# Hybrid decoder step on one core: seven block products in place of eight for gate and up in the first and the last FFN phase

## The chip, the core and the metric

The kernel runs on one core of a Trainium2 chip. The metric is device time in microseconds (us) of one execution, given as the median of several runs. TensorE multiplies, VectorE, ScalarE and GpSimd work element by element, and DMA engines move data between HBM and SBUF; SyncE issues nearly all transfers.

## The reference, cut to what is computed

One layer for 1024 prompt rows and 8 single-token rows (samples), model width 1024, FFN width 2816, all in fp32. Both groups share the weights.

```python
def swiglu(x, w_gate, w_up, w_down):
    return (jax.nn.silu(x @ w_gate) * (x @ w_up)) @ w_down

def decoder_layer(x, ...):
    h = x + 0.5 * rmsnorm(swiglu(rmsnorm(x, n_ffn1_pre), ffn1_gate, ffn1_up, ffn1_down), n_ffn1_post)
    proj = rmsnorm(h, n_mix_pre) @ w_in
    ya = ...      # differential attention with a paged cache for the samples
    yb = ...      # RWKV-7 time mixing
    h = h + rmsnorm(jnp.concatenate([ya, yb], axis=-1) @ w_out, n_mix_post)
    h = h + 0.5 * rmsnorm(swiglu(rmsnorm(h, n_ffn2_pre), ffn2_gate, ffn2_up, ffn2_down), n_ffn2_post)
    return h, k, v, s_new, shift_new
```

## The kernel before

**Phases.** Activations lie transposed: model or FFN columns on the partitions, rows (tokens) along the free axis. The two FFNs times two halves of the rows give four phases, `ph` 0 to 3: FFN 1 on the first 520 and on the last 512 rows, then FFN 2 on the other two. Phases 0 and 3 stand at the start and at the end of the span and work on two chunks of 256 and 264 rows; phases 1 and 2 take 512 rows at a time and share the middle of the span with projections, attention and time mixing, which other streams supply.

**One product.** Fp32 accuracy comes from splitting: each operand is a high part (rounded to fp32r) and a low part (the rest), and `mm3` issues three fp32r matmuls per block of 128 rows of the weight: high x high, high x low, low x high. A gate or up product of one column tile (128 of the 2816 columns, `f` = 0 to 21) sums over 8 such blocks, 24 matmuls per chunk.

**Weights.** The stream `s_weights` loads a column tile of 512 KB into one of two raw buffers (`wts_raw`), and `split` makes the high part with a cast on ScalarE and the low part with a subtraction on VectorE or GpSimd: `either` takes the one that by the planner's prices is free first. The parts go into one of four buffers `w0` to `w3` (`wts_w` in the trace) in phases 0 and 3, after the signal `used` of the buffer's last tenant. `plan` gives the sequence: groups of two or three column tiles, gate and up for each tile, and behind the first tile of a group the down products of the group before.

**The trunk.** `s_trunk` runs the products. In `gate`, ScalarE takes tanh(g/2) of the PSUM result and VectorE forms g(1 + tanh); `up` multiplies by the up product, ScalarE casts the high part, `either` makes the low part. In phase 0 the input is not yet normalized: the gate result is multiplied by `rb` (the reciprocal norm of each row) on VectorE before the tanh, and g once more by `rb` on GpSimd, so that the up product gets its norm too. `down` sums over the tiles of a group and adds into `ytile` (`trunk_xl` in the trace). The last group of a phase is its tail: with each result, `square_sum` adds up the squares for the norm behind the FFN, and in phase 3 `s_end` turns the results back and writes them out.

**Order.** Each engine's instructions are ordered before the kernel runs by a list scheduler (`Kern.run`): streams offer their next instruction, `price` costs it, and the one with the earliest latest-start time (`late`, from a dry pass, plus `BIAS` of its stream) goes first. The order is fixed in the program; on the chip each engine follows it and waits on semaphores. The fences of rows below show pieces of that order.

## Time and profile before

| | before |
|---|---|
| median of 3 runs | 2362.34 us (2361.39 to 2362.57) |
| the profiled execution | 2372.71 us |
| span of its instructions | 2371.0 us |
| mean granted TensorE clock | 0.983 |
| TensorE busy | 2284.7 us, 96% |
| VectorE busy | 1432.8 us, 60% |
| ScalarE busy | 1012.4 us, 43% |
| GpSimd busy | 913.6 us, 39% |

The trace and its rows come from the one profiled execution; its time holds the span and 1.7 us around it. The granted clock is a share of full speed, 1.00 being 2.4 GHz. A busy TensorE is not TensorE at its peak, and a share over the whole span averages phases with different limits. In a trace `trunk` names the FFN trunk, `wts` its weights, `mix` the time mixing, `end` the output, `pre` the split inputs; a name such as `trunk_m` is a PSUM bank.

### The profile page before, as it was taken

To read this page: it belongs to the slowest core of one execution; us is meant where nothing else is said; L and a number is where in the kernel's file an instruction comes from. 1 tells how busy PE (TensorE), PEld (TensorE's weight loads), DVE (VectorE), ACT (ScalarE), POOL (GpSimd) and SP (SyncE) were. 2 spreads that over 40 slices of the span, in tenths; PEclk is the share of its full clock that TensorE was granted. 3 is DMA by queue.
4 is the path that set the end of the run, shared out by engine and by line. 5 is a ranking of instruction groups with operands and counts; after the bars stand their busy time and mean duration, and the time that the engine had idled before them with its cause. 6 is when DMAs were issued, how large, how long until landed. Compare 5 with 4: busy or idle time off the path is not lost.

```text
span 2371.0 us, 42298 instructions
## 1 busy us (share of the span) xinstructions
PE 2284.7 (96%) x16207; PEld 2039.5 (86%) x16207; DVE 1432.8 (60%) x3118; ACT 1012.4 (43%) x1967; POOL 913.6 (39%) x735
## 2 busy tenths in 40 slices
PE   7999999999999999999799989999999999999998
PEld 7999999898887777888788867777778989999998
DVE  5554445856667876648866567555677576334444
ACT  5532223544453245444542154443575564322224
POOL 4542222533433864445642133333443464111112
PEclk9999999999999999999889999999999999999999
DMA  6332233444343664635546942323544535322332
GB/s 206 121 96 88 87 93 112 140 140 132 108 125 109 205 204 138 182 114 167 149 132 182 203 113 76 90 72 92 154 140 119 172 97 146 111 84 87 91 97 73
DMA packets 461698, 299.09 MB, mean 126 GB/s; under 512 B 81177, under 2 KB 428925, under 8 KB 461496
## 3 DMA queue, kind: packets, MB, share of 16 engines
q1 hardware_dynamic: 460888, 294.78, 42.9%
q8 instruction: 128, 2.10, 0.4%
q0 software_dynamic: 320, 1.08, 0.1%
q14 instruction: 74, 0.61, 0.1%
q10 hardware_dynamic: 288, 0.52, 0.1%
HBM read 254.86 MB, written 41.46 MB: 125 GB/s over the span
## 4 chain that ended last, share of the span: by engine, by line
PE 79%; DVE 8%; ACT 5%; DMA 4%; issue 2%; POOL 1%; SPq 1%; DVEq 0%; ACTq 0%; POOLq 0%
PE trunk_m L296 50%; PE proj_m L296 10%; PE trunk_aux L296 5%; PE job_aux L296 4%; PE outb_m L296 2%; PE attn_m L296 2%; PE out_m L296 2%; DVE mix_T L296 1%; PE attn_aux L296 1%; ACT mix_X L296 1%; SPq L296 1%; ACT wts_w L296 1%; ACT mix_T L296 1%; DVE trunk_xl L296 1%; PE job_dec L296 1%
## 5 line engine op out<-in xcount | busy, mean ns | idle before, releaser
L296 PE MATMUL trunk_m<-pre_X,wts_w 128*128 128x256 f32 (+2 forms) x3264 | 556.4, 325 | 8.9 <-ACT pre_sq L296 3.5
L296 PEld LDWEIGHTS trunk_m<-pre_X,wts_w 128*128 128x128 f32 x3264 | 462.3, 193 | 50.0 <-issue 5.5
L296 PE MATMUL trunk_m<-trunk_xl,wts_w 128*128 128x256 f32 (+2 forms) x2856 | 475.6, 320 | 13.5 <-DVE trunk_xl L296 10.7
L296 ACT CAST wts_w<-wts_raw 128x1024 fp32r<-128x1024 f32 (+1 forms) x288 | 281.4, 978 | 441.6 <-PE trunk_m L296 343.9
L296 POOL TENSOR_TENSOR wts_w<-wts_raw,wts_w 128x1024 fp32r<-128x1024 f32 (+1 forms) x130 | 293.7, 2259 | 450.4 <-ACT wts_w L296 368.4
L296 PE MATMUL trunk_m<-pre_T,wts_w 128*128 128x256 f32 (+2 forms) x2592 | 452.9, 329 | 8.5 <-DVE wts_w L296 6.9
L296 PEld LDWEIGHTS trunk_m<-trunk_xl,wts_w 128*128 128x128 f32 x2856 | 403.9, 191 | 51.4 <-DVE trunk_xl L296 13.7
L296 PEld LDWEIGHTS trunk_m<-pre_T,wts_w 128*128 128x128 f32 x2592 | 375.0, 189 | 47.6 <-DVE wts_w L296 7.7
L296 DVE TENSOR_TENSOR trunk_xl<-trunk_xl,trunk_m 128x256 f32<-128x256 f32 (+2 forms) x314 | 155.8, 502 | 122.7 <-PE trunk_m L296 121.9
L296 DVE TENSOR_TENSOR wts_w<-wts_raw,wts_w 128x1024 fp32r<-128x1024 f32 (+1 forms) x158 | 185.9, 1176 | 68.8 <-ACT wts_w L296 68.0
L296 POOL TENSOR_TENSOR trunk_xl<-trunk_t,trunk_xl 128x256 fp32r<-128x256 f32 (+2 forms) x90 | 98.8, 1098 | 267.6 <-ACT trunk_xl L296 267.4
L296 PE MATMUL proj_m<-tail_xl,lin_w 128*128 128x256 f32 (+1 forms) x1248 | 165.1, 287 | 0.0
L296 PEld LDWEIGHTS proj_m<-tail_xl,lin_w 128*128 128x128 f32 x1248 | 153.5, 188 | 7.7 <-issue 6.1
L296 PE MATMUL proj_m<-tail_T,lin_w 128*128 128x512 f32 (+1 forms) x672 | 153.2, 388 | 4.8 <-DVE tail_T L296 4.8
L296 PEld LDWEIGHTS proj_m<-tail_T,lin_w 128*128 128x128 f32 x672 | 123.5, 195 | 32.7 <-DVE tail_T L296 5.5
L296 ACT CAST trunk_xl<-trunk_t 128x256 fp32r<-128x256 f32 (+2 forms) x131 | 61.2, 467 | 112.0 <-DVE trunk_t L296 68.1
L296 POOL TENSOR_TENSOR trunk_g<-trunk_g,init_rb 128x256 f32<-128x256 f32 (+1 forms) x44 | 41.3, 939 | 126.6 <-ACT trunk_t L296 126.6
L296 DVE TENSOR_TENSOR trunk_t<-trunk_g,trunk_m 128x512 f32<-128x512 f32 (+2 forms) x78 | 43.4, 557 | 76.0 <-PE trunk_m L296 73.5
L296 DVE SCALAR_TENSOR_TENSOR trunk_g<-trunk_t,trunk_m 128x512 f32<-128x512 f32 (+2 forms) x78 | 43.4, 557 | 72.8 <-ACT trunk_t L296 72.5
L296 PE MATMUL trunk_aux<-pre_T,wts_w 128*128 128x264 f32 (+1 forms) x672 | 86.8, 284 | 0.0
L296 PEld LDWEIGHTS trunk_aux<-pre_T,wts_w 128*128 128x128 f32 x672 | 83.4, 189 | 0.1
L296 POOL TENSOR_TENSOR mix_T<-mix_T 128x512 f32<-128x512 f32 x32 | 38.0, 1189 | 89.1 <-DMA mix_T<-PT 89.1
(497 smaller groups left out, 3469.9 us busy)
## 6 DMA issues: line engine op xcount, KB each, us to landing
wts_raw<-in_ffn_gate_dram SPq DMA_DIRECT2D x88, 512.0 KB
wts_raw<-in_ffn_up_dram SPq DMA_DIRECT2D x88, 512.0 KB
wts_raw<-in_ffn_down_dram SPq DMA_DIRECT2D x96, 384.0 KB
lin_raw<-in_w_in_dram SPq DMA_DIRECT2D x26, 512.0 KB
mix_T<-PT SPq DMA_DIRECT2D x37, 256.0 KB
wts_raw<-in_ffn_down_dram SPq DMA_DIRECT2D x16, 512.0 KB
dec_dreg<-in_cache_k_dram SPq DMA_DIRECT2D x32, 256.0 KB
dec_dreg<-in_cache_v_dram SPq DMA_DIRECT2D x32, 256.0 KB
```

The source lines that it names most:

```text
L296: o = Op(eng, lambda: fn(*a, **k), st)
```

## The change

`FAST = {0: 10, 3: 6}`: from column tile 10 of phase 0 and tile 6 of phase 3 on, two neighbouring tiles are a pair, and gate and up of a pair are done as a 2x2 block product with seven block multiplications (Strassen's form as Winograd wrote it). The blocks are the two tiles (a11, a12 the halves of the first over the 1024 rows of the weight, a21, a22 of the second) and the input by halves of the model width and by two halves of 260 rows. A block product is 4 blocks of 3 matmuls of 260 columns. Five streams change:

- `s_combine`, new, forms four sums of input blocks per phase: 40 additions or subtractions, 16 casts and 16 low parts of 260 columns, into `dreg`, `T2` and `T3`.
- `s_weights`: a pair's two tiles are loaded as before; `sums` makes from them four fillings of a weight buffer per kind, the first with a11 and a12, the second with the sums s2 and a11 - a21, the third with a22 and s1, the fourth (half full) with a12 - s2. s1 and s2 are written by VectorE to the PSUM banks `cb` and `dec`. Raw buffers come in two pairs in turn (`four`). All casts and low parts of the fast downs and of the sums are of 512 columns (`PARTS = 2`).
- `seven`, new: the seven products and their 14 additions per pair on VectorE, gate and up element work on blocks of 260 rows. The trunk has six PSUM banks there.
- Groups: phase 0 has [0,1,2], [3,4], [5,6,7], [8,9] and six pairs, phase 3 [0,1,2], [3], [4,5] and eight pairs. Before, both ended with a group of three.
- Phase 0 no longer multiplies g by `rb` on GpSimd. The FFN's output then lacks one factor of `rb` per row, which the norm behind it takes out, but for its epsilon: squares are scaled by `TINY`, and `s_tail` multiplies by `rb` three times on VectorE.
- `BIAS` has new values for streams of the middle as well.

```diff
+FAST = {0: 10, 3: 6}
+HALF = 260
...
-BIAS = {"trunk2": 300, "outn3": -60, "outb0": 30, "pre2": -3}
+BIAS = {"trunk2": 300, "outn3": -70, "outb0": 30, "pre2": 7, "prep1": 60, "resid0": -60, "outn1": -10, "pre3": 30, "outn0": 3, "pre1": 3, "job13": 60, "ldxb0": -60}
...
+    def sums(self, ph, kind, f, j, tag, last):
...
+        if tag in last:
+            yield ("wait", last[tag])
+        hl = self.T(self.wp, [P, 2048], tag, FR)
...
+        elif j == 1:
+            s1, s2 = self.ps(bank="cb"), self.ps(bank="dec")
+            V.tensor_tensor(s1, a21, a22, ALU.add)
+            V.tensor_tensor(s2, s1, a11, ALU.subtract)
+            put(0, s2)
+            V.tensor_tensor(a12, a12, s2, ALU.subtract)
+            self.either("tensor_tensor", a11, a11, a21, ALU.subtract)
+            put(1, a11)
+            ab.append(s1)
...
-                    G.tensor_tensor(g, g, rb, ALU.mult)
...
+                    for n, (j, i, x) in enumerate(((0, 0, b11), (0, 1, b21), (1, 0, t2), (1, 1, t3), (2, 0, t4), (2, 1, t1), (3, 0, b22))):
+                        wh, wl = yield from weights(kind, f, j)
+                        ps = self.ps(HALF)
+                        for k in range(4):
+                            self.mm3(ps, wh[:, i, k, :], wl[:, i, k, :], x[0][k], x[1][k], k == 0, k == 3)
...
+                        if n == 0:
+                            A.copy(v[0], ps)
+                        elif n == 5:
+                            V.tensor_tensor(v[2], v[2], ps, ALU.add)
+                            V.tensor_tensor(v[0], v[0], ps, ALU.add)
+                        else:
+                            o, a = ((1, 0), (0, 0), (2, 0), (3, 2), (0, 0), (0, 0))[n - 1]
+                            V.tensor_tensor(v[o], v[a], ps, ALU.add)
...
+        if ph == 0:
+            rb = self.rb[:, o:o + n]
+            for _ in range(2):
+                nc.vector.tensor_tensor(acc, acc, rb, ALU.mult)
+        self.rstd(acc, 2, 1.0 if ph else TINY ** -2)
+        if ph == 0:
+            nc.vector.tensor_tensor(acc, acc, rb, ALU.mult)
```

The order on TensorE, in the last phase before the change: the end of the down products of a group and the first rows of a gate product. `pre_T` is the input, its two numbers the high and the low part; `trunk_m` a PSUM bank; one weight filling (`wts_w_2632`) serves both chunks.

```order
L296 MATMUL trunk_aux_2648_23843<-trunk_xl_837_7957,wts_w_2626_23663 128x264 x9
L296 MATMUL trunk_m_2649_23854<-trunk_xl_837_7957,wts_w_2626_23663 128x256 x9
L296 MATMUL trunk_m_2652_23868<-pre_T_2188_19398,wts_w_2632_23716 128x264
L296 MATMUL trunk_m_2652_23868<-pre_T_2189_19399,wts_w_2632_23716 128x264
L296 MATMUL trunk_m_2652_23868<-pre_T_2188_19398,wts_w_2632_23716 128x264 x2
L296 MATMUL trunk_m_2652_23868<-pre_T_2189_19399,wts_w_2632_23716 128x264
```

And after it, for a pair: each block product is 12 matmuls on half a filling of the weights (`comb` is a sum of input blocks, `pre_T` a block of the input itself).

```order
L301 MATMUL trunk_m_2747_23058<-comb_dreg_20421,wts_w_2731_22949 128x260 x12
L301 MATMUL trunk_m_2748_23077<-comb_T_2435_20422,wts_w_2731_22949 128x260 x12
L301 MATMUL trunk_aux_2752_23097<-comb_T_2436_20423,wts_w_2737_22988 128x260 x12
L301 MATMUL trunk_aux_2753_23114<-comb_dreg_20421,wts_w_2737_22988 128x260 x12
L301 MATMUL trunk_m_2755_23138<-pre_T_2321_19678,wts_w_2740_23009 128x260
L301 MATMUL trunk_m_2755_23138<-pre_T_2322_19679,wts_w_2740_23009 128x260
L301 MATMUL trunk_m_2755_23138<-pre_T_2321_19678,wts_w_2740_23009 128x260 x2
```

A filling of a weight buffer that served 48 matmuls of gate or up serves 24 (12 for the fourth) behind the change.

The order on VectorE in the last phase before: three additions of down products, then gates, the low parts of weight fillings (1024 columns), and ups.

```order
L296 TENSOR_TENSOR trunk_xl_1556_14256<-trunk_xl_1556_14256,trunk_m_2593_23269 128x256
L296 TENSOR_TENSOR trunk_xl_1556_14256<-trunk_xl_1556_14256,trunk_m_2594_23281 128x264
L296 TENSOR_TENSOR trunk_xl_1556_14256<-trunk_xl_1556_14256,trunk_aux_2595_23292 128x256
L296 SCALAR_TENSOR_TENSOR trunk_g_23327<-trunk_t_23328,trunk_m_2598_23306 128x264
L296 SCALAR_TENSOR_TENSOR trunk_g_23327<-trunk_t_23328,trunk_m_2601_23337 128x256
L296 TENSOR_TENSOR wts_w_2602_23358<-wts_raw_23301,wts_w_2602_23358 128x1024
L296 TENSOR_TENSOR trunk_t_23328<-trunk_g_23327,trunk_aux_2604_23368 128x264
L296 TENSOR_TENSOR trunk_xl_837_7957<-trunk_t_23328,trunk_xl_837_7957 128x264
L296 TENSOR_TENSOR trunk_t_23328<-trunk_g_23327,trunk_m_2605_23398 128x256
L296 TENSOR_TENSOR wts_w_2606_23419<-wts_raw_23359,wts_w_2606_23419 128x1024
L296 SCALAR_TENSOR_TENSOR trunk_g_23450<-trunk_t_23451,trunk_m_2608_23430 128x264
```

And after, where one pair's downs end and the next pair's gates begin: `rows_X` and `init_E` are the places in which block products are summed, `wts_cb` and `wts_dec` the PSUM banks of s1 and s2.

```order
L301 TENSOR_TENSOR trunk_xl_1702_14632<-trunk_xl_1702_14632,trunk_aux_2887_24143 128x256
L301 TENSOR_TENSOR rows_X_2366_20050<-rows_X_2366_20050,trunk_m_2894_24172 128x260
L301 TENSOR_TENSOR wts_w_2895_24179<-wts_lraw_24145,wts_w_2895_24179 128x512
L301 TENSOR_TENSOR rows_X_2366_20050<-rows_X_2366_20050,trunk_m_2896_24187 128x260
L301 TENSOR_TENSOR wts_cb_24216<-wts_LT_24146 128x512
L301 SCALAR_TENSOR_TENSOR trunk_g_24156<-trunk_sq_24195,rows_X_2366_20050 128x260
L301 TENSOR_TENSOR wts_dec_24217<-wts_cb_24216,wts_lraw_24145 128x512
L301 TENSOR_TENSOR init_E_109<-rows_X_2366_20050,trunk_m_2898_24207 128x260
L301 TENSOR_TENSOR init_E_109<-init_E_109,trunk_m_2902_24227 128x260
L301 TENSOR_TENSOR wts_w_2899_24215<-wts_dec_24217,wts_w_2899_24215 128x512
L301 TENSOR_TENSOR wts_lraw_24145<-wts_lraw_24145,wts_dec_24217 128x512
L301 TENSOR_TENSOR init_E_109<-init_E_109,trunk_aux_2903_24244 128x260
```

In place of one low part of 1024 columns to a filling there are sums and low parts of 512, and between them stand the additions of the block products.

The order on TensorE at the end of the program, where the last group's down products are interleaved with the transposes of the output (`end`); before, a group of three tiles, 9 matmuls to a result:

```order
L296 MATMUL trunk_m_2673_24116<-trunk_xl_837_7957,wts_w_2656_23920 128x264 x9
L296 MATMUL trunk_m_2676_24130<-trunk_xl_837_7957,wts_w_2656_23920 128x264 x9
L296 MATMUL trunk_aux_2678_24144<-trunk_xl_837_7957,wts_w_2660_23981 128x264 x9
L296 MATMUL trunk_m_2680_24158<-trunk_xl_837_7957,wts_w_2660_23981 128x264 x5
L296 MATMUL end_m_2674_24123<-init_ident_69,trunk_xl_1556_14256 128x128
L296 MATMUL end_aux_2675_24124<-init_ident_69,trunk_xl_1556_14256 128x128
L296 MATMUL trunk_m_2680_24158<-trunk_xl_837_7957,wts_w_2660_23981 128x264
L296 MATMUL end_m_2674_24123<-init_ident_69,trunk_xl_1556_14256 128x128
L296 MATMUL end_aux_2675_24124<-init_ident_69,trunk_xl_1556_14256 128x128
```

And after, a group of two tiles, 6 matmuls to a result:

```order
L301 MATMUL trunk_aux_2999_24993<-trunk_xl_978_8303,wts_w_2977_24810 128x264 x6
L301 MATMUL trunk_m_3002_25004<-trunk_xl_978_8303,wts_w_2977_24810 128x264 x6
L301 MATMUL trunk_m_3004_25015<-trunk_xl_978_8303,wts_w_2977_24810 128x264 x6
L301 MATMUL trunk_aux_3006_25029<-trunk_xl_978_8303,wts_w_2977_24810 128x264 x3
L301 MATMUL end_m_3000_24994<-init_ident_69,trunk_xl_1702_14632 128x128
L301 MATMUL end_aux_3001_24995<-init_ident_69,trunk_xl_1702_14632 128x128
L301 MATMUL trunk_aux_3006_25029<-trunk_xl_978_8303,wts_w_2977_24810 128x264 x3
L301 MATMUL trunk_m_3008_25040<-trunk_xl_978_8303,wts_w_2980_24833 128x264 x2
L301 MATMUL end_m_3000_24994<-init_ident_69,trunk_xl_1702_14632 128x128
```

The transposes stand behind the same number of results, with fewer matmuls between them.

## Rows read from the trace of the kernel before

**Rows 1.** The page's parts 1 and 2: busy time in us, share of the span and count of instructions of each engine, and then busy tenths of TensorE and the granted TensorE clock in 40 equal slices of the span.

```profile
PE 2284.7 (96%) x16207; PEld 2039.5 (86%) x16207; DVE 1432.8 (60%) x3118; ACT 1012.4 (43%) x1967; POOL 913.6 (39%) x735
...
PE   7999999999999999999799989999999999999998
...
PEclk9999999999999999999889999999999999999999
```

**Rows 2.** Windows: stretch in us from the start of the span and its length, busy us of TensorE, of its weight loads, of VectorE, ScalarE and GpSimd with the count of instructions, then mean granted clock, mean DMA share and GB/s. The first two lie in the first FFN phase, the others in the last; windows left out between them read alike.

```profile
200.00:260.00 60.00, 60.00 (x504) 60.00 (x503) 27.79 (x54) 16.96 (x26) 14.35 (x14) 1.00 0.32 94
260.00:320.00 60.00, 60.00 (x501) 60.00 (x501) 27.00 (x54) 16.36 (x24) 15.69 (x13) 1.00 0.31 94
...
2100.00:2160.00 60.00, 60.00 (x500) 59.88 (x498) 26.65 (x51) 14.89 (x24) 10.72 (x8) 1.00 0.30 89
2280.00:2340.00 60.00, 60.00 (x501) 60.00 (x500) 21.62 (x43) 15.28 (x26) 10.69 (x8) 1.00 0.26 82
```

**Rows 3.** The chain that ended last, in order of time, near the end of the span: start in us, us, engine, what is written, line, and the count of instructions in the piece.

```profile
2323.86 5.77 PE trunk_m L296 x48
2329.63 2.92 PE trunk_aux L296 x24
2332.55 5.75 PE trunk_m L296 x48
2338.31 2.84 PE trunk_aux L296 x24
```

**Rows 4.** Windows of the middle of the span, columns as in rows 2.

```profile
480.00:800.00 320.00, 314.17 (x2698) 273.02 (x2697) 208.22 (x627) 136.60 (x275) 125.86 (x98) 1.00 0.45 129
800.00:1120.00 320.00, 308.49 (x1647) 256.01 (x1645) 216.93 (x460) 139.28 (x290) 177.98 (x125) 0.98 0.55 165
1120.00:1200.00 80.00, 65.58 (x427) 61.78 (x427) 63.66 (x124) 41.71 (x80) 44.55 (x47) 0.81 0.48 135
1200.00:1520.00 320.00, 304.05 (x1768) 237.23 (x1766) 203.33 (x428) 125.13 (x215) 105.69 (x72) 0.98 0.55 141
1520.00:1840.00 320.00, 311.47 (x1926) 251.13 (x1926) 217.34 (x588) 164.18 (x399) 121.89 (x78) 0.99 0.40 112
```

**Rows 5.** The timeline of VectorE alone in the last phase: start us, duration us, engine, line, operation, out<-in, shapes, and in brackets the idle time before it and what ended it.

```profile
2105.66 1.22 DVE L296 TENSOR_TENSOR wts_w<-wts_raw,wts_w 128x1024 fp32r<-128x1024 f32 x1
2106.80 0.41 DVE L296 TENSOR_TENSOR trunk_xl<-trunk_xl,trunk_aux 128x256 f32<-128x256 f32 x1
2107.13 0.76 DVE L296 TENSOR_TENSOR trunk_xl<-trunk_xl,trunk_m 128x264 f32<-128x264 f32 x2
2108.31 0.43 DVE L296 TENSOR_TENSOR trunk_xl<-trunk_xl,trunk_aux 128x264 f32<-128x264 f32 x1 [0.42 <-PE trunk_aux L296]
```

**Rows 6.** Groups of instructions over the whole span, shapes kept apart: engine, operation, names, shapes, count, then busy us and mean ns of one, then the idle time before them and what ended it.

```profile
L296 DVE TENSOR_TENSOR trunk_xl<-trunk_xl,trunk_m 128x512 f32<-128x512 f32 x96 | 65.4, 683 | 51.5 <-PE trunk_m L296 51.1
L296 DVE TENSOR_TENSOR mix_T<-mix_T 128x512 f32<-128x512 f32 x24 | 19.4, 807 | 2.8 <-ACT mix_T L296 2.8
L296 DVE SCALAR_TENSOR_TENSOR mix_T<-mix_T,setup_cols,mix_T 128x512 f32<-128x512 f32 x24 | 22.7, 946 | 1.2 <-POOL mix_T L296 1.2
L296 POOL TENSOR_TENSOR mix_T<-mix_T 128x512 f32<-128x512 f32 x32 | 38.0, 1189 | 89.1 <-DMA mix_T<-PT 89.1
L296 POOL TENSOR_TENSOR trunk_xl<-trunk_t,trunk_xl 128x512 fp32r<-128x512 f32 x31 | 44.6, 1439 | 45.2 <-ACT trunk_xl L296 45.0
L296 ACT CAST trunk_xl<-trunk_t 128x512 fp32r<-128x512 f32 x37 | 22.8, 617 | 3.7 <-DVE trunk_t L296 3.6
```

**Rows 7.** The same view of GpSimd alone, 2040 to 2340 us.

```profile
L296 POOL TENSOR_TENSOR trunk_xl<-trunk_t,trunk_xl 128x256 fp32r<-128x256 f32 x12 | 15.9, 1322 | 51.3 <-ACT trunk_xl L296 51.3
L296 POOL TENSOR_TENSOR trunk_xl<-trunk_t,trunk_xl 128x264 fp32r<-128x264 f32 x14 | 10.6, 757 | 130.0 <-ACT trunk_xl L296 130.0
```

**Rows 8.** The same view of ScalarE alone, 2040 to 2340 us.

```profile
L296 ACT CAST trunk_xl<-trunk_t 128x264 fp32r<-128x264 f32 x18 | 7.4, 413 | 40.8 <-DVE trunk_t L296 40.8
L296 ACT ACTIVATE trunk_t<-trunk_m 128x264 f32<-128x264 f32 x13 | 5.1, 392 | 22.9 <-PE trunk_m L296 14.9 <-POOL trunk_xl L296 8.0
```

**Rows 9.** Timelines of ScalarE and of GpSimd in the last phase, columns as in rows 5: two casts of a weight's high part, and the low part that GpSimd makes after the second.

```profile
2104.57 1.06 ACT L296 CAST wts_w<-wts_raw 128x1024 fp32r<-128x1024 f32 x1 [4.53 <-PE trunk_m L296]
2110.47 1.05 ACT L296 CAST wts_w<-wts_raw 128x1024 fp32r<-128x1024 f32 x1 [4.84 <-PE trunk_aux L296]
...
2111.60 2.38 POOL L296 TENSOR_TENSOR wts_w<-wts_raw,wts_w 128x1024 fp32r<-128x1024 f32 x1 [10.00 <-ACT wts_w L296]
```

**Rows 10.** TensorE's waits, by what released it: us in total, times, longest us. These are the three rows in which a weight's parts were waited for.

```profile
PE trunk_m L296 <- DVE wts_w L296: 9.8, 5, 4.6
PE trunk_m L296 <- POOL wts_w L296: 1.3, 1, 1.3
PE trunk_m L296 <- ACT wts_w L296: 0.8, 2, 0.4
```

**Rows 11.** The first piece of the chain that ended last.

```profile
1.96 6.36 DMA wts_raw<-in_ffn_gate_dram
```

**Rows 12.** A window over the last group of down products (its first matmul starts at 2341.14), columns as in rows 2.

```profile
2341.14:2363.50 22.36, 22.29 (x189) 21.63 (x187) 13.03 (x29) 16.89 (x37) 9.06 (x12) 1.00 0.14 49
```

**Rows 13.** Windows near the start of the span, and behind the end of the first phase.

```profile
40.00:90.00 50.00, 48.80 (x404) 48.16 (x404) 23.04 (x53) 25.93 (x52) 19.75 (x21) 0.99 0.58 194
440.00:480.00 40.00, 40.00 (x244) 35.71 (x243) 30.54 (x38) 25.61 (x49) 19.96 (x21) 1.00 0.43 129
```

More of the change, by code (lines that the diff above doesn't have):

```diff
@@ L557, in split @@
         h, l = (hl[:, 1024 * j:1024 * j + n] for j in range(2))
-        self.nc.scalar.copy(h, raw)
-        self.either("tensor_tensor", l, raw, h.bitcast(F32), ALU.subtract)
+        for i in range(0, n, n // parts):
+            t = slice(i, i + n // parts)
+            self.nc.scalar.copy(h[:, t], raw[:, t])
+            self.either("tensor_tensor", l[:, t], raw[:, t], h[:, t].bitcast(F32), ALU.subtract)
         return [t.rearrange("p (a b) -> p a b", a=a) for t in (h, l)]
@@ L772, in plan @@
             for q, f in enumerate(grp):
-                seq += [("gate", f, None), ("up", f, None)]
+                if f < FAST.get(ph, NF):
+                    seq += [("gate", f, None), ("up", f, None)]
+                elif q == 0:
+                    seq += [(kind, f, j) for kind in ("gates", "ups") for j in range(4)]
                 if gi and q == 0:
@@ L798, in s_weights @@
                     yield ("wait", ("outw", 1))
-                raw = self.raw()
+                if kind[-1] == "s":
+                    yield from self.sums(ph, kind, f, m0, tag, last)
+                    continue
+                fast = kind == "down" and groups[f][-1] + 1 >= FAST.get(ph, NF + 1)
+                if fast and not FOUR:
+                    self.side = 1
+                raw = self.four(m0 // 512) if fast else self.raw()
                 w = I[f"ffn{1 + ph // 2}_{kind}"]
@@ L924, in s_trunk @@
                 for q, f in enumerate(grp):
+                    if f >= FAST.get(ph, NF):
+                        if q == 0:
+                            if f == FAST[ph]:
+                                yield ("wait", ("combined", ph))
+                                self.cur.banks = tuple(f"m{j}" for j in range(4)) + ("aux0", "aux1")
+                                rest = [self.rest[:, HALF * i:HALF * i + HALF] for i in range(4)] if ph else [r[:, i, :] for _ in range(2) for r in [self.residual(HALF)] for i in range(2)]
+                                self.vs = [t[:, HALF * i:HALF * i + HALF] for t in (self.E, self.prb) for i in range(2)] + [self.la[:, :HALF], self.sg[:, :HALF]] + rest
+                                self.nv = 0
+                            yield from seven(f)
+                            yield from down(gi - 1, False)
+                        continue
                     if ph == 1 and f == LEAD:
@@ L954, in s_pre @@
             if c == 0:
-                x = self.x[ph] = self.parts(ph, *self.two(half))
+                tiles = self.two(half)
+                x = self.x[ph] = self.parts(ph, *tiles)
+                self.xt[ph] = [t.rearrange("p (k t) -> p k t", t=520) for t in tiles]
             for k in range(KT):
```

178 lines of the change are left out of this document (152 added, 26 removed).

## The prediction

> **What bounds the kernel now.** I read four views in this order. The page's busy shares and slices come first: TensorE is busy 96% of the span and VectorE 60% [rows 1], and the slices say where TensorE is not full. Then windows over the two stretches that the change touches: in the first FFN phase (here 200 to 380 us) and in the last (2040 to 2340 us) TensorE is busy 60.00 of every 60 us at full granted clock, VectorE 22 to 28, ScalarE 15 to 17, GpSimd 10 to 16, the DMA engines about 0.3 [rows 2]. Third, the chain that ended last runs there through matmuls alone, 48 and 24 at a time without a piece of another engine between [rows 3]. So in both stretches the end is set by the count of matmuls, and a matmul that goes away is worth its issue interval. Fourth, the middle: between 480 and 1840 us TensorE is idle 56 of 1360 us, and the granted clock falls below full where it idles [rows 4]; the change does not edit that part, but its order moves.
>
> **What is removed.** A pair of FFN column tiles had 2 tiles x 2 products x 8 blocks of rows x 3 passes x 2 chunks = 192 matmuls for gate and up; seven block products of 4 x 3 matmuls, twice, are 168. There are 6 pairs in the first phase (tiles 10 to 21) and 8 in the last (6 to 21): 14 x 24 = 336 matmuls less, all of 260 columns on average as before. Down products keep their count. From rows 3, 5.77 + 2.92 + 5.75 + 2.84 = 17.28 us for 144 matmuls is 0.120 us each, so 336 are **40.3 us**, as long as TensorE stays full.
>
> **What has to keep up, per pair.** TensorE needs 168 + 96 down matmuls = 264 x 0.120 = 31.7 us for a pair (34.6 before).
>
> VectorE: in the new order of the last phase there stand, per pair, 16 instructions of 512 columns (weight sums and low parts) and 39 of 256 to 264 columns (14 additions of block products, 16 down evictions, 4 gates, 4 ups, a low part). Back to back it starts the next instruction 1.14 us after one of 1024 columns and 0.33 us after one of 256 [rows 5], so about 1.05 ns a column: 0.60 us for 512. That is 16 x 0.60 + 39 x 0.34 = 23 us; by mean durations (0.68 and 0.81 us for 512 [rows 6], 0.43 for the small ones [rows 5]) it is at most 16 x 0.81 + 39 x 0.43 = 30 us. The first phase has four more small ones (1.4 us). GpSimd has about 10.7 instructions of 512 columns and 3.2 of 260 a pair: 10.7 x 1.19 to 1.44 [rows 6] + 3.2 x 0.76 to 1.32 [rows 7] = 15 to 20 us. ScalarE has 18.6 casts of 512 at 0.62 [rows 6] and 10 short ones of about 0.4 [rows 8]: 16 us. All are under 31.7, so no engine but TensorE is full; VectorE at its upper bound is close.
>
> No row shows VectorE writing PSUM, which 4 sums a pair now do. From below it is the 0.68 us of a 512-column addition that reads PSUM, from above the slowest VectorE row of 512 columns, 0.95 us [rows 6]. I take 0.68, since the operands are as many; the upper end adds 4 x 0.27 = 1.1 us of VectorE a pair, which the 31.7 us cover; without cover 15 us in all.
>
> **The weight buffers turn faster.** Four buffers are refilled in turn. Before, three others stood between (3 x 48 matmuls = 17 us); now they are 24, 24 and 12 matmuls at the tightest, 60 x 0.120 = 7.2 us. A refill ran from release to ready in 2.3 us where VectorE made the low part (cast starts at 2104.57, low part ends at 2106.88) and in 3.5 us with GpSimd (2110.47 to 2113.98) [rows 5, 9]. Now there are two casts and two low parts of half the size, for the second buffer also a sum in front: 2.9 to 5 us. That fits into 7.2 with 2 to 4 us for queueing. Before, TensorE waited 11.9 us in all for weights [rows 10], over 288 refills 0.041 us each; 140 refills at that rate are **5.8 us**, which I take, between 0 and the 20 us that 0.14 us each would make. The loads behind them are the same bytes; DMA is at a third [rows 2], a load at the crowded start landed in 6.4 us [rows 11], and a pair of raw buffers is asked for some 11 us before its use. Nothing for it.
>
> **The ends.** The last group of down products had three tiles, now two: the tail's matmuls drop from 144 to 96, 5.8 us that move ahead and are not lost. But in the 22.4 us of that tail ScalarE was busy 16.9 us and TensorE 22.3 [rows 12]. TensorE's share falls to 16.5, so ScalarE's 16.9 plus the wait for the first sum and its gaps (about 2 us) sets the end: 19 in place of 16.5, **+2.5 us** (0 to 4). At the end of the first phase three multiplications by rb of 0.43 us join the path to the residual; the next phase's first products fill it as now (40.00 of 40 us busy after 440 [rows 13]), so nothing, or 1.3 us without that cover. GpSimd's multiplication of the gate by rb goes, and nothing waited for it in [rows 2].
>
> Forming the four sums of x takes 56 additions and 16 casts of 260 columns a phase, 24 us if all 56 were VectorE's at 0.43, in stretches where both are under half busy and TensorE full, ahead of tile 10 and tile 6. Nothing, as long as it ends by then; in the first phase eight of these instructions come in the first 90 us, where TensorE is not full [rows 13]: 0 to 3 us, taken as 0 since TensorE waits there for others.
>
> **The middle.** New BIAS values reorder it. I take 0, with 10 us either way: one stretch, 1120 to 1200 us, alone has 14.4 us of idle TensorE and a mean clock of 0.81 [rows 4], and so much can be won or lost by an order.
>
> **The sum.** The profiled execution took 2372.71 us (span 2371.0 and 1.7 around it), 10.4 above the median of 2362.34. 2372.7 - 40.3 + 5.8 + 2.5 = 2340.7 for such an execution; less 10.4, **2330 us**.
>
> **A rule that speaks against it.** GpSimd's subtraction of 264 columns takes 0.76 us in the last phase, the same on 256 columns 1.32 [rows 7]: the second kind falls together with VectorE's 1.22 us weight subtraction, and stretches. The Trainium skill, SBUF — State Buffer, section SBUF: two separate sides, says that VectorE with two SBUF inputs and GpSimd exclude each other for a whole instruction; by that rule, and the stretched row agrees, the new mix would cost waiting on both engines. Taken as a mechanism of this kernel it is the second rival below.
>
> **Rivals.**
> (a) *Refills come late.* If a refill is late by 0.14 to 0.25 us on average, 20 to 35 us of the 40 are lost: 2344 to 2359. For it: 7.2 us in place of 17, a fixed order on VectorE. Against: at least 2 us to spare.
> (b) *VectorE and GpSimd block each other and VectorE becomes the bound; slower.* Per pair GpSimd holds 15 us, VectorE needs 23, of which 17 instructions (about 8 us) have two SBUF inputs. If VectorE stood still for more than 34.6 - 23 = 11.6 us of GpSimd's 15, a pair would take longer than before. At 13 us a pair takes 36 us, 1.4 x 14 = 20 us over before: 2382. Against: 15 + 8 = 23 us of exclusive work fit into 31.7, and only those 8 us of VectorE can be held.
> (c) *The middle pays or costs.* A gain of 10 us beside no stall: 2312; a loss of 10 to 20 there: 2340 to 2350.
> (d) *The matmuls go, time does not*: another chain sets the phases. Rows 2 and 3 exclude it but for a few per cent: about 2362.
>
> **Chances.** Forecast (2320 to 2341) 0.60; (a) 0.13; (b) 0.05; (c) better than 2320 0.12, worse than 2341 0.07; (d) 0.03. No change that can be told is within 0.2%, 4.7 us. Faster: 0.60 + 0.13 + 0.12 + 0.07 less 0.03 for the far ends of (a) and (c), 0.89; same 0.04; slower 0.07. The range from 2314 (all 40 us and a share of the middle) to 2350 (most of (a) and (c)) leaves about 2 in 10 out.
>
> **What would show it.** Right: windows in both phases still read 60 of 60 us for TensorE with about 500 matmuls; VectorE at 44 to 55 of 60; TensorE's waits for weights grow by under 10 us; the last phase from tile 6 on is some 23 us shorter, the first 17. Wrong: TensorE below 58 of 60 there, its idle time ended by the weight sums' low parts (a); VectorE near 60 of 60 with GpSimd's 512-column rows above 2 us (b); both phases shorter as said but the middle longer (c).

## The result: 2347 us, half of the gain that was forecast

The changed kernel takes 2346.96 us (median of 6 runs, 2337.83 to 2351.05) against 2362.45 (6 runs) before: ratio 0.9931, 95% interval 0.9909 to 0.9953. The forecast was 2330 with a range of 2314 to 2350; the gain is 15.5 us in place of 32. Its profiled execution took 2346.93 us, like the median; that of before, 2372.71, stood 10.3 above this one.

The page of the changed kernel, part 1:

```profile
PE 2247.0 (96%) x15871; PEld 1996.0 (85%) x15871; DVE 1658.5 (71%) x3616; ACT 1078.9 (46%) x2182; POOL 1069.0 (46%) x868
```

Beside [rows 1] there are 336 matmuls less, and VectorE has risen from 60% to 71%. I cut the span at two marks on TensorE: the first matmul of the second FFN phase, and that of the last. The windows between the marks (columns as in rows 2), before and then after:

```profile
0.00:415.19 415.19, 400.43 (x3269) 397.07 (x3269) 209.67 (x402) 162.25 (x285) 146.34 (x143) 0.99 0.37 115
415.19:1971.29 1556.10, 1492.60 (x9690) 1252.13 (x9688) 1046.18 (x2409) 719.53 (x1457) 681.68 (x521) 0.98 0.48 136
1971.29:2371.00 399.71, 391.65 (x3252) 390.31 (x3252) 176.91 (x309) 130.62 (x226) 85.56 (x72) 1.00 0.33 100
```

```profile
0.00:406.91 406.91, 385.00 (x3125) 379.90 (x3125) 313.58 (x613) 191.60 (x382) 211.36 (x181) 0.99 0.40 119
406.91:1964.84 1557.93, 1492.58 (x9687) 1248.69 (x9688) 1055.78 (x2417) 715.16 (x1451) 676.51 (x522) 0.98 0.48 135
1964.84:2345.10 380.26, 369.46 (x3060) 367.44 (x3060) 289.13 (x587) 172.11 (x351) 181.14 (x165) 0.99 0.36 105
```

The first stage is 8.3 us shorter, with 144 matmuls less; 17.3 were forecast. The last is 19.4 shorter with 192 less; 23.0 less 2.5 were forecast. The middles of the two profiled executions are nearly equal. But if the first and the last stage take in a median execution what they take in the trace (e1 below has 414.5 and 399.7), the middle of before takes 2362.45 - 1.7 - 415.2 - 399.7 = 1545.9 us there, and after the change 1558.1: 12 us are lost. No trace of a median execution of before exists. -8.3 - 19.4 + 12.2 = -15.5.

Windows of the changed kernel while the pairs run, two of the first phase and two of the last (answering to [rows 2]):

```profile
200.00:260.00 60.00, 59.40 (x492) 58.98 (x491) 53.06 (x109) 24.56 (x51) 32.26 (x27) 1.00 0.35 97
260.00:320.00 60.00, 59.07 (x491) 58.86 (x490) 51.54 (x105) 27.04 (x55) 35.25 (x29) 1.00 0.37 106
...
2080.00:2140.00 60.00, 60.00 (x502) 60.00 (x501) 48.03 (x106) 26.02 (x52) 29.56 (x27) 1.00 0.38 105
2200.00:2260.00 60.00, 60.00 (x502) 60.00 (x501) 47.44 (x105) 27.11 (x55) 28.86 (x26) 1.00 0.37 106
```

The last phase is what was forecast: TensorE 60.00 of 60, VectorE 47 to 48, GpSimd 29, ScalarE 24 to 27. In the first phase VectorE stands at 52 to 53 and TensorE has gaps.

TensorE's waits for a weight's parts, over the whole span (answering to [rows 10]):

```profile
PE trunk_m L301 <- POOL wts_w L301: 1.8, 2, 1.5
PE trunk_m L301 <- DVE wts_w L301: 1.4, 2, 1.0
PE trunk_m L301 <- ACT wts_w L301: 0.5, 1, 0.5
```

The faster turn of the weight buffers costs nothing: 3.7 us in all, 11.9 before; in the first and the last stage alone 1.9, 3.1 before.

### The profile page after: what moved, and what is told of

Its sections match the earlier page's. It is cut to its first block, busy times and chain, and to the rows that moved or that the text cites. A ratio compares the mean times of both kernels' runs of the same rounds, so it can differ in the third digit from the quotient of the medians.

```text
span 2345.1 us, 42680 instructions
## 1 busy us (share of the span) xinstructions
PE 2247.0 (96%) x15871; PEld 1996.0 (85%) x15871; DVE 1658.5 (71%) x3616; ACT 1078.9 (46%) x2182; POOL 1069.0 (46%) x868
## 4 chain that ended last, share of the span: by engine, by line
PE 58%; DVE 8%; ACT 3%; DMA 2%; issue 2%; POOL 1%; SPq 1%; DVEq 0%; POOLq 0%; ACTq 0%
PE trunk_m L301 32%; PE proj_m L301 7%; PE trunk_aux L301 5%; PE job_aux L301 4%; PE out_m L301 2%; PE outb_m L301 2%; PE attn_m L301 2%; PE attn_aux L301 2%; DVE mix_T L301 1%; DVE job_st L301 1%; DMA dec_dreg<-in_cache_k_dram 1%; DVE trunk_xl L301 1%; PE job_dec L301 1%; SPq L301 1%; DVE dec_dreg L301 1%
## 5 line engine op out<-in xcount | busy, mean ns | idle before, releaser
L301 POOL TENSOR_TENSOR wts_w<-wts_raw,wts_w 128x1024 fp32r<-128x1024 f32 (+2 forms) x184 | 349.5, 1905 | 372.9 <-ACT wts_w L301 296.6
L301 PE MATMUL trunk_m<-trunk_xl,wts_w 128*128 128x256 f32 (+2 forms) x2670 | 454.5, 322 | 12.1 <-DVE trunk_xl L301 10.3
L301 PE MATMUL trunk_m<-pre_X,wts_w 128*128 128x512 f32 (+3 forms) x2400 | 447.7, 336 | 11.3 <-ACT pre_sq L301 3.3
L301 PEld LDWEIGHTS trunk_m<-pre_X,wts_w 128*128 128x128 f32 x2400 | 353.6, 191 | 53.5 <-issue 7.0
L301 PE MATMUL trunk_m<-pre_T,wts_w 128*128 128x512 f32 (+3 forms) x1920 | 372.7, 345 | 3.3 <-DVE trunk_xl L301 2.3
L301 ACT CAST wts_w<-wts_raw 128x1024 fp32r<-128x1024 f32 (+2 forms) x293 | 247.0, 855 | 272.1 <-PE trunk_m L301 187.1
L301 PEld LDWEIGHTS trunk_m<-pre_T,wts_w 128*128 128x128 f32 x1920 | 296.1, 190 | 42.0 <-issue 3.3
L301 POOL TENSOR_TENSOR trunk_xl<-trunk_t,trunk_xl 128x512 fp32r<-128x512 f32 (+3 forms) x79 | 86.4, 1095 | 126.7 <-ACT trunk_xl L301 126.3
L301 DVE TENSOR_TENSOR wts_w<-wts_raw,wts_w 128x1024 fp32r<-128x1024 f32 (+2 forms) x109 | 117.9, 1089 | 23.7 <-ACT wts_w L301 23.1
L301 PE MATMUL trunk_aux<-trunk_xl,wts_w 128*128 128x256 f32 (+1 forms) x546 | 75.9, 284 | 0.4 <-DVE trunk_xl L301 0.4
L301 PEld LDWEIGHTS trunk_aux<-trunk_xl,wts_w 128*128 128x128 f32 x546 | 69.7, 189 | 0.6 <-DVE trunk_xl L301 0.6
L301 ACT CAST wts_w<-wts_lraw 128x512 fp32r<-128x512 f32 x88 | 51.9, 620 | 39.4 <-PE trunk_m L301 15.5
```

The lines of the kernel that those rows point to most:

```text
L301: o = Op(eng, lambda: fn(*a, **k), st)
```

## The experiments

The stages of all runs, cut as above from their profiled executions (us), and the medians of the timed runs with their ratio to the kernel before, timed beside them. A profiled execution lies within 4 us of its median, but for the first trace of before (10.3 above) and e5 (9.2 above):

| run | median | ratio (95%) | first | middle | last |
|---|---|---|---|---|---|
| before, first trace | 2362.45 | | 415.2 | 1556.1 | 399.7 |
| e1_before_again | one run, 2369.17 | | 414.5 | 1553.2 | 399.7 |
| after | 2346.96 | 0.9931 (0.9909 to 0.9953) | 406.9 | 1557.9 | 380.3 |
| e2_last_only | 2377.62 | 1.0051 (1.0033 to 1.0069) | 415.2 | 1579.5 | 381.2 |
| e3_first_only | 2368.33 | 1.0021 (1.0005 to 1.0038) | 408.3 | 1562.5 | 399.1 |
| e4_old_bias | 2374.00 | 1.0040 (1.0025 to 1.0055) | 407.1 | 1585.0 | 380.6 |
| e5_new_bias_alone | 2379.21 | 1.0064 (1.0042 to 1.0086) | 418.9 | 1568.9 | 398.8 |
| e6_tail_four | 2375.02 | 1.0049 (1.0036 to 1.0063) | 420.3 | 1569.4 | 382.9 |
| e7_tail_four_no_single | 2375.56 | 1.0053 (1.0031 to 1.0074) | 418.6 | 1570.3 | 384.3 |
| e8_no_rb_in_gates | one run, 2350.69 | | 400.0 | 1559.8 | 389.0 |
| e9_rb_on_gpsimd | 2352.67 | 0.9961 (0.9942 to 0.9979) | 409.9 | 1560.5 | 380.3 |
| e10_old_middle | 2344.00 | 0.9926 (0.9904 to 0.9947) | 410.0 | 1552.2 | 380.7 |
| e11_split_gates | 2338.24 | 0.9888 (0.9868 to 0.9907) | 404.4 | 1551.7 | 383.6 |
| e12_split_and_four | 2344.73 | 0.9929 (0.9907 to 0.9951) | 406.1 | 1544.1 | 393.3 |

**The parts apart.** e1 is the kernel before, without an edit.

> The kernel before once more, unchanged, for a second trace of it. The first stage is the span up to the first matmul of the second FFN phase, the middle from there to the first matmul of the last FFN phase, the last stage from there to the end of the span: 415.2, 1556.1 and 399.7 us in the first trace, 406.9, 1557.9 and 380.3 us after the change. Theory A (the profiled execution of before lost its 10 us over the median in the middle, by chance): 415, 1546 and 400 here, and so the change costs about 12 us in the middle. Theory B (a profiled execution of before takes that long): 1556 again in the middle, and the difference of the traces, 26 us, overstates the gain.

The middle took 1553 us, in an execution that was again above the median: neither 1546 nor a proof that a profiled execution is always long. What the executions differ in stands in the last section.

```diff
-FAST = {0: 10, 3: 6}
+FAST = {3: 6}
```

> The changed kernel with the seven block products in the last phase alone; the first phase has its eight products and groups again, with the new way of using rb and the new BIAS. Theory A (the stages pay each for itself, and the middle does not depend on the first phase's products): first stage about 415, middle about 1558, last 380, 2355 us in all. Rival C (the order of the middle changes with all that stands ahead of it): the last stage 380 as well, but the middle off by up to 15 us either way, so 2340 to 2370.

```diff
-FAST = {0: 10, 3: 6}
+FAST = {0: 10}
```

> The changed kernel with the seven block products in the first phase alone. Theory A: first stage 407, middle 1558, last 400, 2366 us in all, which is no gain over the kernel before: what the first phase wins the middle loses. Rival C: first 407 and last 400, the middle off by up to 15 us either way, 2351 to 2381.

First and last stage came as A had them, each for itself; the middle did not keep still, as C had it: 1579.5 without the first phase's products, 21 us more and not the 15 that C allowed. Either part alone is slower than the kernel before, by 0.5 and 0.2%. With old products in the first phase and the new use of rb (e2) the first stage is 415.2 as before, so rb's three multiplications at its end cost nothing there.

```diff
-BIAS = {"trunk2": 300, "outn3": -70, "outb0": 30, "pre2": 7, "prep1": 60, "resid0": -60, "outn1": -10, "pre3": 30, "outn0": 3, "pre1": 3, "job13": 60, "ldxb0": -60}
+BIAS = {"trunk2": 300, "outn3": -60, "outb0": 30, "pre2": -3}
```

> The changed kernel with the four BIAS values of the kernel before. Theory D (the new BIAS costs the middle the missing 12 us): middle about 1546, 2335 us in all. Rival E (the new values were needed because the middle's order changes with what stands ahead of it): the middle the same or longer, 2347 to 2365. First stage 407 and last 380 by both.

e5 is the reverse edit on the kernel before:

> The kernel before with the new BIAS values and nothing else. Theory E (a set of values fits one order; the middle's time hangs on the whole order and on the granted clock in it): first stage 415, last 400, the middle longer than the 1547 us that it takes in a median execution of before, by 5 to 40 us: 2367 to 2400 in all. Rival D (the new values order the middle better, whatever stands around it): 2335 to 2355.

D falls twice, and E went further than its own 2365 us. With the old values the changed kernel's middle takes 1585 us and the gain is gone; with the new ones the kernel before is 16 us slower, 4 of them in the first stage, whose order moved too. A set of values fits one order: the new one took 27 us out of the middle that the change had put in.

**The end of the first phase.** TensorE's timeline there in the changed kernel, and a window behind it:

```profile
399.26 1.73 PE L301 MATMUL trunk_aux<-trunk_xl,wts_w 128*128 128x264 f32 x12 [0.40 <-DVE trunk_xl L301]
404.47 0.70 PE L301 MATMUL tail_dec<-trunk_acc,init_onesD 128*128 128x256 f32 x2 [1.30 <-DVE trunk_acc L301]
406.91 14.12 PE L301 MATMUL trunk_m<-pre_T,wts_w 128*128 128x256 f32 x96 [1.74 <-DVE trunk_xl L301]
```

```profile
406.91:420.86 13.95, 13.95 (x96) 13.95 (x97) 10.17 (x17) 4.93 (x10) 8.82 (x10) 0.80 0.11 39
```

3.4 us of idle time, ended by VectorE's work; then the granted clock is at the 1.2 GHz level for part of the next 14 us (0.80 on average), and 96 matmuls take 13.95 us where [rows 3] give 11.5. The same stretch before, and after:

```profile
380.00:415.19 35.19, 35.19 (x294) 35.07 (x292) 17.85 (x36) 14.88 (x28) 11.61 (x13) 1.00 0.36 114
```

```profile
380.00:406.91 26.91, 22.86 (x184) 21.86 (x182) 19.98 (x45) 10.61 (x21) 11.86 (x12) 0.98 0.58 176
```

What VectorE does while `tail_dec`, the matmul that sums the squares for the norm, waits 1.30 us for `trunk_acc`, are two of the multiplications by rb:

```profile
403.06 1.35 DVE L301 TENSOR_TENSOR trunk_acc<-trunk_acc,init_rb 128x256 f32<-128x256 f32 x2
```

```diff
-            groups = {0: [[0, 1, 2], [3, 4], [5, 6, 7], [8, 9]], 3: [[0, 1, 2], [3], [4, 5]]}[ph] + [[g, g + 1] for g in range(FAST[ph], NF, 2)]
+            groups = {0: [[0, 1, 2], [3, 4], [5, 6, 7], [8, 9]], 3: [[0, 1, 2], [3], [4, 5]]}[ph] + [[g, g + 1] for g in range(FAST[ph], NF - 4, 2)] + [list(range(NF - 4, NF))]
...
-        return {1: 8, 2: 4, 3: 2}[len(grp)]
+        return {1: 8, 2: 4, 3: 2, 4: 2}[len(grp)]
```

> The changed kernel with the last two pairs of both phases in one group of four tiles, so that the last down products have 12 matmuls to a result in place of 6; the count of matmuls is the same. Theory T (with 6 matmuls, 0.72 us, to a result the tail is paced by VectorE, ScalarE and GpSimd; TensorE's 3.4 us of idle time there bring the clock down right behind it): no idle TensorE in the first phase's tail, full clock behind it, the first stage 402 to 404 in place of 406.9, the first 96 matmuls behind it 11.5 us in place of 14.0, the last stage 377.5 to 379 in place of 380.3. Rival U (the wait at the first phase's end comes from the three multiplications by rb): the first stage stays at 406 to 407. The middle is expected to move by up to 15 us either way, as in the runs so far: 2325 to 2355 in all, 2338 if it holds.

Missed: 420.3, outside what T and U had. TensorE's timeline of that run:

```profile
294.05 3.95 PE L301 MATMUL trunk_m<-trunk_xl,wts_w 128*128 128x256 f32 x18 [2.14 <-DVE trunk_xl L301]
362.04 3.94 PE L301 MATMUL trunk_m<-trunk_xl,wts_w 128*128 128x256 f32 x18 [1.92 <-DVE trunk_xl L301]
394.91 0.38 PE L301 MATMUL trunk_m<-trunk_xl,wts_w 128*128 128x256 f32 x1 [2.65 <-ACT trunk_xl L301]
395.74 4.87 PE L301 MATMUL trunk_m<-trunk_xl,wts_w 128*128 128x256 f32 x26 [0.45 <-POOL trunk_xl L301]
```

The tail starts right behind its own pair and waits 3.1 us for its activations, and the new order made the waits between pairs worse, 2 us each. A third part stands ahead of the pairs: the windows of the first 60 us, in the changed kernel and here,

```profile
0.00:60.00 60.00, 43.85 (x301) 41.02 (x302) 41.14 (x72) 34.92 (x66) 30.96 (x30) 0.91 0.63 200
```

```profile
0.00:60.00 60.00, 39.36 (x252) 35.81 (x253) 38.86 (x70) 34.04 (x63) 27.35 (x28) 0.86 0.61 196
```

have 301 and 252 matmuls, 5.9 us of work apart: in the new order TensorE waits 4.7 and 4.2 us for VectorE at two places where it waited 2.9 and 1.5. At the phase's end itself T was right: 0.5 us of idle time in place of 3.4, with all the multiplications by rb done, and the granted clock at 1.00 behind it (420.33 to 440). In the last phase the tail paid what it promised at its end (9.2 us from the last down product to the end, 12.3 after the change) and lost 3.1 at its start.

```diff
-            groups = {0: [[0, 1, 2], [3, 4], [5, 6, 7], [8, 9]], 3: [[0, 1, 2], [3], [4, 5]]}[ph] + [[g, g + 1] for g in range(FAST[ph], NF - 4, 2)] + [list(range(NF - 4, NF))]
+            groups = {0: [[0, 1, 2], [3, 4], [5, 6, 7], [8, 9]], 3: [[0, 1, 2], [3, 4, 5]]}[ph] + [[g, g + 1] for g in range(FAST[ph], NF - 4, 2)] + [list(range(NF - 4, NF))]
```

> As the run with the group of four, and the last phase's groups 3 and 4, 5 made one group of three. Theory T2 (a group of a single tile gives 3 matmuls, 0.36 us, to a result, less than the 0.42 us of its addition on VectorE, so TensorE waits there): the four waits of 1.8 us in all near the start of the last phase go, and 8 us of VectorE's additions with them; the last stage 375.5 to 377.5. Rival: those waits come from forming the sums of the input, which fall into the same stretch; then the last stage is that of the run with the group of four.

In this kernel tile 7's activations take tile 3's place in the ring of four before the group's down products read it; the work is the same in amount, but what it writes is not the layer's output. In the changed kernel the four waits were these (two of them):

```profile
2046.91 0.99 PE L301 MATMUL trunk_m<-trunk_xl,wts_w 128*128 128x256 f32 x6 [1.01 <-DVE trunk_xl L301]
2048.52 0.98 PE L301 MATMUL trunk_m<-trunk_xl,wts_w 128*128 128x264 f32 x6 [0.26 <-DVE trunk_xl L301]
```

They are gone, though the sums of the input are still formed there, which speaks for T2 as to the cause. Two waits of 2.3 us in all for activations stand in their place, ahead of the group's first down products, and the last stage gained nothing (384.3, 382.9 with the group of four). Those down products read tile 7's activations, made just before them, so the waits may come from that exchange: what T2 is worth in time this run does not show.

**VectorE in the first phase.**

```diff
-                    if ph == 0:
-                        V.tensor_tensor(g, src, self.rb[:, HALF * j:HALF * j + HALF], ALU.mult)
-                        src = g
```

> As the run with the group of four, but the gates of the first phase's pairs leave the multiplication by rb out, so that the gate works on products that are not normalized. Theory V (in the first phase VectorE, at 53 of 60 us with its rows stretched by GpSimd, is what TensorE waits for between pairs): VectorE's share in the first phase's pairs falls by about 3 us to a pair, to 47 or 48 of 60 us, and TensorE's idle time of 2.3 us there goes; the first stage 2 to 3 us under that of the run with the group of four. Rival: the waits come from the order and stay.

A window in its pairs:

```profile
260.00:320.00 60.00, 60.00 (x501) 60.00 (x500) 47.32 (x105) 25.93 (x53) 29.18 (x25) 1.00 0.38 106
```

Without the 24 multiplications TensorE is full from 140 to 410 us, even at the end of the phase with its group of four: 400.0 us, 15 of the 17.3 that were forecast. Of the 20 us between this run and e6, 4.9 stand in the first 60 us (293 matmuls against 252), ahead of all pairs; the order was made anew. For the rest the cause hangs on these 24 instructions, or on the order without them. Is it their time, or their place? From here on each stream's instructions keep a recorded order and engine, so that nothing else moves:

```diff
+            heads = {l[0][0] for l in self.lines if l}
...
+                        if o.rank in self.engs and o.rank not in heads:
+                            continue
```

```diff
-                        V.tensor_tensor(g, src, self.rb[:, HALF * j:HALF * j + HALF], ALU.mult)
+                        nc.gpsimd.tensor_tensor(g, src, self.rb[:, HALF * j:HALF * j + HALF], ALU.mult)
```

> The changed kernel with its order on every engine kept as it is, but the 24 multiplications of a gate by rb in the first phase's pairs on GpSimd in place of VectorE. The order of everything else cannot move, so the middle should take what it takes in the changed kernel, about 1558 us. Theory V (VectorE is what TensorE waits for in the first phase's pairs): VectorE falls from 53 to about 49 of 60 us, the waits of 0.2 to 0.9 us behind each pair go, the first stage 404 to 405.5 in place of 406.9, 2344.5 in all. Rival W (GpSimd's instruction, 0.75 us where VectorE's is 0.42, lengthens the gate's path and blocks VectorE for longer): the waits stay or grow, the first stage 407 to 412. The end of the phase with its 3.4 us of idle TensorE is the same in both.

W holds: 409.9. VectorE's waits for the tanh (`trunk_sq`) between 200 and 385 us, in the changed kernel, and in e9:

```profile
DVE trunk_t L301 <- ACT trunk_sq L301: 5.6, 8, 1.5
...
DVE trunk_g L301 <- ACT trunk_sq L301: 1.6, 3, 0.5
```

```profile
DVE trunk_t L308 <- ACT trunk_sq L308: 16.6, 10, 3.3
...
DVE trunk_g L308 <- ACT trunk_sq L308: 4.7, 5, 2.3
```

VectorE is less busy (48 of 60) and yet late: it stands for a tanh whose input has just been made. The first phase's gate has one step more ahead of its tanh than the last phase's, which takes the sum itself.

Then the rest of the order (lines against e9, cut):

```diff
-    late, seq = order(False)
...
-    nc = build(late, False, [seq])
+    late, seq = order(False)
+    _, was = order(True)
+    mine = [x for x in seq if x[0][0] in HELD]
+    rest = [x for x in was if x[0][0] not in HELD]
+    nc = build(late, False, [mine, rest])
```

`order(True)` plans the kernel before, `HELD` names the trunk, weights, sums, tails and output of phases 0 and 3; rb's multiplication is on VectorE again.

> The changed kernel in which all streams but those of the first and last phase's trunk, weights, sums, tails and output keep among themselves the order and the engines that they have in the kernel before; the others keep theirs of the changed kernel; the two are merged by the planned times. Theory M (the order of the middle, made anew with other BIAS values, costs the 11 us between a median execution's middle of before, 1547 us, and that of the changed kernel, 1558): middle 1545 to 1552, first stage 407, last 380, 2335 to 2341 in all. Rival N (the middle is longer because of the state in which the first phase hands over, its clock and the late VectorE, not because of the order): 1556 to 1562 again, 2345 to 2351.

The middle of a median execution is 2344.0 - 1.7 - 410.0 - 380.7 = 1551.6 us, at the upper edge of what M had and under what N had; 6.5 of the 12 are back. The total, 2344.0, lies between the two, for the first stage lost 3 in the merging. So the total gains 3, which is less than the intervals can tell (0.2%, 5 us, to either side).

```diff
-                    V.scalar_tensor_tensor(g, t, 1.0, src, ALU.add, ALU.mult)
+                    if SPLIT and ph == 0:
+                        then.append((step[0] + LAG, V.scalar_tensor_tensor, g, t, 1.0, src, ALU.add, ALU.mult))
+                    else:
+                        V.scalar_tensor_tensor(g, t, 1.0, src, ALU.add, ALU.mult)
```

`LAG` is 3 block products; the tanh is written over the sum and no longer into `trunk_sq`. The first phase's streams are planned anew, the rest is held as in e10.

> As the run with the old order in the middle, and in the first phase's pairs VectorE's second instruction of a gate, g(1 + tanh), stands three block products behind the multiplication by rb that feeds the tanh, in place of right behind it; all the work is done. Theory X (VectorE's order makes it stand still for a tanh on ScalarE whose input it has written one instruction earlier: 7 us of such waits between 200 and 385 us in the changed kernel, 21 us with the multiplication on GpSimd; the additions of down products queue up behind it until TensorE finds no free bank): these waits fall under 2 us, TensorE's waits between pairs go, the first stage 404 to 407 in place of 410.0, what is left being the phase's end. Rival Y (VectorE is simply too full with 53 of 60 us, and only work that is left out helps): VectorE's waits for the tanh fall, TensorE's waits stay, the first stage 408 to 411. Middle 1550 to 1554 and last 380 in both: 2338 to 2342 by X, 2343 to 2347 by Y.

X holds for the first stage and the total, and Y falls by one row:

```profile
260.00:320.00 60.00, 60.00 (x502) 60.00 (x501) 53.67 (x109) 26.81 (x56) 37.02 (x30) 1.00 0.37 107
```

VectorE is as busy as in the changed kernel, 53.67 of 60, and TensorE has 60.00. One wait of 1.1 us between pairs is left, none of VectorE's for a tanh is (between 200 and 385 us no instruction g(1 + tanh) has idle time before it). The first stage is 404.4 and the middle 1551.7, both as X had them; the last is 383.6 for 380. With 2338.24 us this version beats both kernels: 24.8 us under the kernel before beside it.

The first phase's order is new here as well. What speaks for the place and not for a lucky order: the next run has another new order with the same split, and is as full,

```profile
200.00:260.00 60.00, 60.00 (x501) 60.00 (x501) 50.63 (x106) 25.76 (x53) 31.43 (x27) 1.00 0.35 97
260.00:320.00 60.00, 60.00 (x501) 60.00 (x501) 52.73 (x109) 27.59 (x56) 34.21 (x29) 1.00 0.38 106
```

while both orders without it, that of the changed kernel (59.40 and 59.07) and that of e6 (59.34 and 57.86), have gaps. The split and the new place of the tanh's result were not tried apart.

```diff
-    SPLIT, TAIL4 = True, ()
+    SPLIT, TAIL4 = True, (0,)
```

> As the run before it, and the first phase ends with a group of four tiles; the last phase keeps its pairs. Theory X: with the backlog on VectorE gone the group of four starts without the 2.7 us wait for its own activations, TensorE stays full to the end of the phase as in the run without rb in the gates, the first stage 399 to 402, full clock behind it, 2330 to 2337 in all. Rival Z (12 matmuls to a result do not help, since the tail of four directly follows its own activations): a wait of 2 to 3 us at the start of the tail, the first stage 404 to 408.

Z, mostly: 406.1, with 1.9 us of waits at the start of the tail (3.1 in e6). But 2.2 us of the 406.1 were lost in the first 60 us, where this order has 276 matmuls and that of e11 294; without them the first stage would be 404, as in e11. The mark between middle and last moved, with waits of TensorE right behind it (1.8 us for a weight, 5.0 for the third phase's output on GpSimd; the 389.0 of e8 has such waits too); middle and last together are 1937.4 us, 1935.3 in e11. So the group of four gave nothing that can be told.

## Why the prediction was half right

**Matmuls.** Right: 336 less, full windows with 502 in 60 us, 0.120 each: 40.3 us of TensorE's work went.

**What has to keep up.** Right for the last phase: VectorE 47.4 of 60 us is 25 us a pair (23 to 30 forecast), GpSimd 15 (15 to 20), ScalarE 13 to 14 (16). The price without a row, VectorE writing PSUM, was 0.68 taken and 0.69 in three of the four sums of a pair; the fourth, with both operands in SBUF and GpSimd beside it, took 1.13, over the upper end of 0.95:

```profile
L301 DVE TENSOR_TENSOR wts_cb<-wts_LT 128x512 f32<-128x512 f32 x7 | 7.9, 1132 | 0.0
...
L301 DVE TENSOR_TENSOR wts_dec<-wts_cb,wts_raw 128x512 f32<-128x512 f32 x7 | 4.8, 692 | 0.0
```

**Refills.** The term of 5.8 us was mis-sized: nothing was lost, rival (a) did not come. Its rate of 0.041 us a refill was the mean over all four phases; 8.8 of the 11.9 us of [rows 10] lay in the middle, whose work the change leaves as it is.

**The ends.** The last phase's tail was sized right: from its first matmul to the end 26.2 us in place of 29.9, that is 3.7 less where 5.8 of matmuls had moved ahead, 2.1 lost, 2.5 forecast. The first phase's end is the step that failed: I weighed only the three multiplications by rb, at nothing or "1.3 us without that cover", and called the next phase's products the cover. They stand behind the norm's matmul in TensorE's fixed order and covered nothing: 3.4 us idle and 2.5 us of lower clock behind it. Of the 3.4, 1.3 are the wait that ends with two of those multiplications. The other 2.1 are waits for VectorE to evict results of 6 matmuls (0.72 us), each of which costs it 0.42 us and, where it adds the square as well, 0.84; it waits there in turn for squares from ScalarE and for GpSimd, so which of the three sets the pace is not shown. That the short groups let both waits through is: with groups of three and the same rb (e2), and with the group of four (e12), the norm's matmul does not wait, in e6 for 0.5 us.

**First phase, pairs.** "Four more small ones (1.4 us)" counted their time and not their place. The stall of 2.2 us between 200 and 385 us comes from VectorE standing in its order for a tanh, by e8, e9, e11 and e12. What forming the sums cost is small: up to 200 us the changed kernel issues 8 matmuls less than the first trace of before and 13 less than e1, 1.0 to 1.6 us, inside the 0 to 3 given (its idle time of 16.2 us there does not tell, with 14.8 and 16.1 in the two executions of before). Counted in matmuls the 9.0 us that the first stage missed are 1.0 there, 3.1 in the pairs (1477 in place of 1503 between 200 and 380 us) and 4.9 at the end (184 matmuls in 26.91 us, which the 294 in 35.19 of before put at 22.0). A group of one tile in the last phase, 3 matmuls to a result against 0.42 us for its addition, cost 1.8 us that I had not looked for.

**The middle.** Taken as 0 with 10 either way; it was 12 us, rival (c) on its bad side, to which 0.07 was given. e10 gives half of it to the order, within its interval. Of the rest 2.5 us are the clock behind the first phase; some 3 us stay open. By the line of the last section the lower clock of the changed kernel's executions (median 0.9835, before beside e1 0.988) goes with some 8 us, an estimate; how much of that the order brings about is not shown.

**Rival (b)**, VectorE and GpSimd blocking each other. The mechanism shows: the second instruction of a gate takes 0.42 us when GpSimd stands idle, and 1.48 when it starts 0.1 us behind an instruction of GpSimd,

```profile
203.25 0.42 DVE L301 SCALAR_TENSOR_TENSOR trunk_g<-trunk_sq,trunk_g 128x260 f32<-128x260 f32 x1
207.96 1.48 DVE L301 SCALAR_TENSOR_TENSOR trunk_t<-trunk_sq,trunk_t 128x260 f32<-128x260 f32 x1
...
204.36 1.30 POOL L301 TENSOR_TENSOR wts_lraw<-wts_lraw,wts_LT 128x512 f32<-128x512 f32 x1 [1.92 <-DVE wts_dec L301]
207.86 1.30 POOL L301 TENSOR_TENSOR wts_w<-wts_LT,wts_w 128x512 fp32r<-128x512 f32 x1
```

and of the 56 gates in pairs the 14 with no GpSimd instruction beside them took 0.41 to 0.43 us, the other 42 0.74 on average. This agrees with the Trainium skill, SBUF — State Buffer, section SBUF: two separate sides, by which, where VectorE has two inputs in SBUF, the one that starts second waits for the whole instruction of the other. The sum s2, with one operand in PSUM, took 0.69 us with and without GpSimd beside it (10 and 18 times). The blocking decided nothing: with VectorE at 53.67 of 60, stretched rows included, TensorE was full in e11.

**The sum.** -40.3 forecast; back came 9.0 in the first stage (17.3 - 8.3), 3.6 in the last (23.0 - 19.4) and 12.2 in the middle, 24.8 in place of 8.3. The result lies in the range of 2314 to 2350 but outside the 2320 to 2341 that was given 0.60, and that it is not further off is luck in part: the 5.8 us set aside for refills were not needed, and paid for a part of what the ends and the middle lost.

## What to carry to other kernels

An engine that is not full can still be late: ask of each instruction in a fixed order what it waits for and what stands behind it, and put a few others between a write and the use of what another engine makes of it. When groups of accumulating matmuls get shorter, set the time of one group against the time of evicting its result, at every end and for the smallest group. And where a scheduler orders everything, a change in one stage is a draw in the others: hold the order of the rest before you judge the change, since here that draw was worth up to 39 us and the change 28.

## What the runs showed of the hardware

One program's time goes with its granted clock. Of 26 executions of the kernel before beside e1 to e4, the one with a mean clock of 0.982 took 2373.24 us, those with 0.989 took 2359.46 to 2363.20; a straight line through all has 1.9 us for each 0.001, with a scatter of some 3 us about it (1.1 for each 0.001 in the 11 beside e11 and e12). That the clock is the cause is not shown: idle time of TensorE lengthens an execution too, and the clock is low where it idles (0.81 in the 80 us of [rows 4] with 14.4 us of idle time). The first trace of before had 0.983, the timed executions of the changed kernel 0.982 to 0.985. So a profiled execution should be set against the clock of the timed ones before two traces are subtracted. In the forecast the 10.4 us cancel: 2330 is 32 us under the median of before, whichever execution the sum starts from.
